# Average pooling on one core: the last two whole-tile stores queued behind the last loads, coarser last parts, and the final wait in a section of its own

## Chip, cores and metric

The kernel runs on one core of a Trainium2 chip. The metric is the device time of one execution in microseconds (us), as a median over several executions. A profile of one execution has a "span", which is 1.7 to 2.4 us shorter than the time. Trace times below are counted from the start of the span. All runs quoted were with a granted clock of 1.0.

## The reference, cut to what matters

```python
# x: 32 x 128 x 256 x 256 float32, kernel_size = 2, stride = 2
for i in range(h_out):
    for j in range(w_out):
        window = x[:, :, 2*i : 2*i + 2, 2*j : 2*j + 2]
        output[:, :, i, j] = np.mean(window, axis=(2, 3))
```

Each output is the mean of four inputs. The kernel reads 1073.74 MB, writes 268.44 MB, and does four operations for each output.

## The kernel before

A "unit" is 128 output rows, one for each partition: 256 KB read and 64 KB written. There are 4096 units. They are handled as 127 whole tiles of 32 units (tiles 0 to 126) and a last tile 127, cut into parts of 16, 8, 4 and 4 units so that the work after the last load is short. SP issues the loads into two input buffers. DVE (VectorE) adds the two rows of each pair, then the two columns. ACT (ScalarE) multiplies by 0.25 and issues the store. There are two result buffers for whole tiles and a third for tile 127.

```python
def take(engine, sem, n=1):            # wait for a semaphore and count it down
    engine.wait_ge(sem, n)
    engine.sem_inc(sem, -n)

def sums(it, dst):                     # DVE: two adds for each tile or part
    dve.tensor_add(out=it[:, :, 0:w], in0=it[:, :, 0:w], in1=it[:, :, w:]).then_inc(halfway)
    take(dve, halfway)
    dve.tensor_add(out=dst, in0=it[:, :, 0:w:2], in1=it[:, :, 1:w:2]).then_inc(summed)

def tile_sums(b):
    take(dve, stored[b], 16)           # the store out of this result buffer has landed
    take(dve, loaded[b], 16)
    sums(ins[b], res[b])
# ... SP: loads of tiles 0 to 126, each when its buffer is free, then:
        for a, b, part in parts:       # tile 127 in parts of 16, 8, 4, 4 units
            sp.dma_start(out=it[:, a:b], in_=...).then_inc(part, 16)
        take(sp, held)                 # tile 126 scaled
        sp.dma_start(out=ot[whole - 1], in_=res[(whole - 1) % 2]).then_inc(tail, 16)
# ... ACT: scale and store of tiles 0 to 125, then:
        take(act, summed)
        scale(res[(whole - 1) % 2], held)
        for a, b, _ in parts:
            take(act, summed)
            scale(dst[:, a:b])
            take(act, scaled)
            act.dma_start(out=..., in_=dst[:, a:b]).then_inc(tail, 16)
        take(sp, tail, 16 * (len(parts) + 2))      # all stores of the end have landed
```

## Time and profile before

| quantity | value | where it is from |
|---|---|---|
| time, median of the first 3 runs | 3103.62 us (3103.59 to 3103.67) | timed runs |
| span of the profiled run | 3101.5 us | page header |
| rate over the span | 433 GB/s | page, DMA part |
| DVE and ACT busy | 54% and 15% | page, part 1 |
| last store issued by ACT | 3095.98 us | timeline |
| last increment of the last store | 3100.42 us | trace's semaphore records |

In the traces a whole-tile load or store is 128 packet records (and 16 of 4 bytes each), and each transfer gives its semaphore 16 increments (those of the last load part of before came from 3089.29 to 3090.51 us). The page counts 16 DMA engines, and I read one increment as the end of one engine's share; "landed" means the sixteenth increment. A "piece" is one packet record of the trace: 64 KB for a whole-tile load and 16 KB for a whole-tile store. The lines are shown in the prediction.

### The profile page before, as it was taken

What the parts mean: (1) busy time and instruction counts of PE and PEld (TensorE: products, weight loads), DVE (VectorE), ACT (ScalarE), POOL (GpSimd) and SP (SyncE); (2) the same over time, 40 slices, a digit from 0 to 9 for tenths busy, and PEclk for the clock granted to TensorE, in tenths of its full rate; (3) what the DMA queues carried; (4) which work ended last, traced back from release to release, by engine and by line L of the source; (5) the groups of instructions that cost most, each with busy time, mean ns of one, the idle gap of its engine ahead of it and who ended that gap; (6) DMA issues with size and microseconds to landing.
All of it is one profiled execution on the core that took longest, in us unless ns stands there. A gap on an engine that the chain in (4) does not pass through costs nothing. (4 is left out here: it accounts for less than half of the span.)

```text
span 3101.5 us, 2614 instructions
## 1 busy us (share of the span) xinstructions
DVE 1679.6 (54%) x262; ACT 464.7 (15%) x132; POOL 0.2 (0%) x4
## 2 busy tenths in 40 slices
DVE  4555555555555555555555555555555555555556
ACT  1111111111111111111111111111111111111111
POOL 0000000000000000000000000000000000000000
DMA  9999999999999999999999999999999999999999
GB/s 416 436 440 426 436 440 426 437 440 424 438 440 423 439 437 425 440 428 434 440 433 430 442 423 436 439 427 440 435 426 437 439 427 436 438 424 439 437 425 416
DMA packets 37728, 1342.19 MB, mean 433 GB/s; under 512 B 4192, under 2 KB 4192, under 8 KB 4576
## 3 DMA queue, kind: packets, MB, share of 16 engines
q1 hardware_dynamic: 19008, 1075.85, 80.1%
q10 hardware_dynamic: 18720, 266.35, 20.1%
HBM read 1073.74 MB, written 268.44 MB: 433 GB/s over the span
## 5 line engine op out<-in xcount | busy, mean ns | idle before, releaser
L87 DVE TENSOR_TENSOR in_tile<-in_tile 128x8192 f32<-128x8192 f32 (+1 forms) x131 | 1113.0, 8496 | 1396.4 <-DVEq L67 1396.4
L97 ACT ACTIVATE res<-res 128x4096 f32<-128x4096 f32 (+1 forms) x131 | 463.5, 3538 | 2594.8 <-ACTq L67 2594.8
L89 DVE TENSOR_TENSOR res<-in_tile 128x4096 f32<-128x4096 f32 (+1 forms) x131 | 566.8, 4327 | 19.2
L97 ACT ACT_TABLE_LOAD x1 | 1.3, 1283 | 36.3 <-ACTq L67 36.3
L234 POOL MEMSET const-bfloat16-1.0<- 128x1 bf16 x1 | 0.1, 101 | 0.0
L234 POOL MEMSET const-uint8-127<- 128x1 uint8 x1 | 0.1, 101 | 0.0
L234 POOL MEMSET const-float32-0.0<- 128x1 f32 x1 | 0.1, 98 | 0.2 <-issue 0.2
L234 POOL MEMSET const-float32-1.0<- 128x1 f32 x1 | 0.1, 98 | 0.0
## 6 DMA issues: line engine op xcount, KB each, us to landing
out_dram<-res ACTq DMA_DIRECT2D x126, 2048.0 KB, 30.8
in_tile<-in_x_dram SPq DMA_DIRECT2D x1, 4096.0 KB, 22.0
in_tile<-in_x_dram SPq DMA_DIRECT2D x1, 2048.0 KB, 27.1
in_tile<-in_x_dram SPq DMA_DIRECT2D x2, 1024.0 KB, 30.0
out_dram<-res SPq DMA_DIRECT2D x1, 2048.0 KB, 11.7
in_tile<-in_x_dram SPq DMA_DIRECT2D x127, 31.5
out_dram<-res ACTq DMA_DIRECT2D x1, 1024.0 KB, 8.1
out_dram<-res ACTq DMA_DIRECT2D x1, 512.0 KB, 6.0
```

The source lines that it names most:

```text
L87: dve.tensor_add(out=it[:, :, 0:w], in0=it[:, :, 0:w], in1=it[:, :, w:]).then_inc(halfway)
L89: dve.tensor_add(out=dst, in0=it[:, :, 0:w:2], in1=it[:, :, 1:w:2]).then_inc(summed)
L97: act.mul(out=dst, in_=dst, mul=0.25).then_inc(done)
L234: nc = _bacc.Bacc("TRN2", target_bir_lowering=False, num_devices=1)
```

## The change

Its intent is to let the last loads through before anything that can wait. The store of tile 125 leaves ACT's queue, and both it and the store of tile 126 stand on SP's queue behind the last loads. Tile 127 comes in parts of 16, 8 and 8. The final wait moves to a second section in which only SP takes part, so the other engines can finish while the stores drain. (A section is a `with tc.tile_critical()` block of the code. SP leaves it only when the other engines have finished in it, as its waits of 9.6 and 1.7 us below show.)

```diff
-    halfway, summed, scaled, held, tail = ...
+    halfway, summed, scaled, tail = ...
+    held = [sem(f"held{k}") for k in range(2)]
...
-        b = rest if rest - a <= 4 else a + (rest - a) // 2
+        b = rest if rest - a <= 8 else a + (rest - a) // 2
...
-        take(sp, held)
-        sp.dma_start(out=ot[whole - 1], in_=res[(whole - 1) % 2]).then_inc(tail, 16)
+        for k, t in enumerate((whole - 2, whole - 1)):
+            take(sp, held[k])
+            sp.dma_start(out=ot[t], in_=res[t % 2]).then_inc(tail, 16)
...
-        for t in range(1 + 2 * pairs, whole - 1):
-            scale_store(t, t % 2, stored[t % 2] if t < whole - 2 else tail)
-        take(act, summed)
-        scale(res[(whole - 1) % 2], held)
+        for t in range(1 + 2 * pairs, whole - 2):
+            scale_store(t, t % 2, stored[t % 2])
+        for k, t in enumerate((whole - 2, whole - 1)):
+            take(act, summed)
+            if k == 0:
+                act.sem_inc(free[t % 2])
+            scale(res[t % 2], held[k])
...
+    with tc.tile_critical():
         take(sp, tail, 16 * (len(parts) + 2))
```

More of the change, by code (lines that the diff above doesn't have):

```diff
@@ L60, in _pool_2x2 @@
     loaded, free, stored = [[sem(f"{n}{b}") for b in range(2)] for n in ("loaded", "free", "stored")]
-    halfway, summed, scaled, held, tail = [sem(n) for n in ("halfway", "summed", "scaled", "held", "tail")]
+    halfway, summed, scaled, tail = [sem(n) for n in ("halfway", "summed", "scaled", "tail")]
+    held = [sem(f"held{k}") for k in range(2)]
     def take(engine, sem, n=1):
```

## The prediction

> **What bounds the kernel now.** I read the page first, its header and the rows of shares.
>
> ```profile
> span 3101.5 us, 2614 instructions
> DVE 1679.6 (54%) x262; ACT 464.7 (15%) x132; POOL 0.2 (0%) x4
> ...
> DMA  9999999999999999999999999999999999999999
> ...
> q1 hardware_dynamic: 19008, 1075.85, 80.1%
> q10 hardware_dynamic: 18720, 266.35, 20.1%
> ```
>
> No compute engine is near full, while the DMA row is full in all 40 slices and the two queues' packet times add up to 100.2% of sixteen DMA engines' span. q1 is the SP queue (loads, and the one store that SP issues), q10 the ACT queue (stores). The kernel must read 1073.74 MB and write 268.44 MB; at the page's 433 GB/s that alone is 3099.7 us. So in the main loop nothing but bytes counts. The change touches only the last 45 us, so the second view is the table by stretches over the end (columns: stretch, its length, busy time of DVE, ACT and POOL, clock, DMA share, GB/s).
>
> ```profile
> 3067.00:3080.00 13.00, 12.29 (x2) 0.00 (x0) 0.00 (x0) 1.00 1.01 435
> 3080.00:3090.00 10.00, 9.71 (x5) 5.53 (x2) 0.00 (x0) 1.00 0.99 423
> 3090.00:3096.00 6.00, 4.84 (x5) 2.32 (x3) 0.00 (x0) 1.00 1.00 427
> 3096.00:3099.00 3.00, 0.00 (x0) 0.00 (x0) 0.00 (x0) 1.00 0.93 371
> 3099.00:3101.50 2.50, 0.00 (x0) 0.00 (x0) 0.00 (x0) 1.00 0.03 11
> ```
>
> The DMA engines stay full to 3099: the end is a drain of queued bytes, too, and not a wait for arithmetic. Third, the timeline of the last instructions, because DVE is busy almost without a gap there and would be the next bound (columns: start, duration, engine, line, operation).
>
> ```profile
> 3067.57 8.69 DVE L87 TENSOR_TENSOR in_tile<-in_tile 128x8192 f32<-128x8192 f32 x1 [9.71 <-DVEq L67]
> ...
> 3084.66 0.35 SPq L126 DMA_DIRECT2D out_dram<-res  x1
> ...
> 3087.53 2.29 DVE L87 TENSOR_TENSOR in_tile<-in_tile 128x2048 f32<-128x2048 f32 x1
> ...
> 3089.96 1.23 DVE L89 TENSOR_TENSOR res<-in_tile 128x1024 f32<-128x1024 f32 x1
> 3091.10 1.22 DVE L87 TENSOR_TENSOR in_tile<-in_tile 128x1024 f32<-128x1024 f32 x1
> 3091.30 1.06 ACT L97 ACTIVATE res<-res 128x1024 f32<-128x1024 f32 x1 [1.67 <-ACTq L67]
> ...
> 3095.25 0.63 ACT L97 ACTIVATE res<-res 128x512 f32<-128x512 f32 x1 [1.34 <-ACTq L67]
> 3095.98 0.34 ACTq L154 DMA_DIRECT2D out_dram<-res  x1
> ```
>
> From the trace's instruction records: DVE's start at 3067.57 waited last for the store of tile 124 out of the same result buffer (its wait passed at 3067.35; the load had landed at 3065.5). From then on it runs through to 3095.13. The parts of the last tile landed at 3080.0, 3085.6, 3088.0 and 3090.5, and DVE took them up at 3080.75, 3087.53, 3091.10 and 3093.08: every part was there 0.7 to 3.1 us early. The last store is issued at 3095.98, its last increment arrives at 3100.42 and the program ends at 3101.48.
>
> [...] in the packet records a 64 KB load piece (2.418 us) and a 16 KB store piece (0.611 us) alternate. Moving a store from ACT's queue to SP's therefore changes its place, not the capacity. [...] Here 15 of the last 16 increments arrive by 3099.8 and the sixteenth at 3100.42: one engine is behind the rest, and that one sets the end. [...]
>
> **The change part by part.**
>
> *Order of the transfers.* Before, the store of tile 125 goes to ACT's queue at 3061.76 and its 16 KB pieces alternate with the last tile's 32 KB and 16 KB load pieces. In the packet records this store runs from 3066.95 to 3080.2. After, it waits on SP's queue behind the loads. It is 8 pieces on each engine, 8 x 0.611 = 4.9 us, so the loads end about 4.9 us sooner (some 3084.6 in place of 3089.5) and the store takes 3084.6 to 3089.5. The store of tile 126, issued at 3084.66 as before, starts at 3089.5 as before. From there on both kernels have the same bytes left. Bytes moved within a full stretch give nothing back: 0 us. The rate doesn't differ either: a 16 KB piece takes 0.611 us as a load and as a store. DVE gains nothing from earlier parts, since it found each one waiting already: 0 us. The start of DVE at 3067.57 hangs on the store of tile 124, which is untouched: 0 us.
>
> *16, 8, 8 for 16, 8, 4, 4.* Pieces get larger. Per engine, sixteen load pieces of 8 KB at 0.309 us (4.95) become eight of 16 KB at 0.611 (4.89), and sixteen store pieces of 2 KB at 0.084 (1.35) become eight of 4 KB at 0.1595 (1.28): together 0.13 us less DMA time by these durations. Successive 2 KB records start 0.08 us apart on the late engine, so the store part may be nearly nothing; I take 0.1 us. On DVE two pairs of adds become one: before 3091.10 to 3095.13; after, 2.43 us to the second add (3089.96 - 3087.53) and 1.225 us of it, so to 3094.76: 0.38 sooner. ACT's last step then takes 1.06 in place of 0.63, and the issue falls at about 3095.98 + 0.43 - 0.38 = 3096.03: 0.05 later. That is beside the drain: the stores ahead of it (the 1 MB and the first 512 KB one) keep the engines busy until about 3097.4, the late engine until 3098.7. An issued transfer needs about 1.0 us to its first packet (the first load: 0.96 to 1.98), with up to 1.8 us on the last of the engines; so its pieces are ready at 3097.05 to 3097.85. On most engines there is no hole, on some one of up to 0.4 us, but the late engine, which sets the end, has none.
>
> *The second section.* Before, after the last increment SP, ACT and DVE go through the exit of the section (3100.50 to 3100.79 in the records), then all engines through the program's end barrier (to 3101.48): 1.06 us. After, ACT and DVE leave the first section while stores are still draining, and after the wait SP has only its own exit. One semaphore step of some 0.07 us and the round trip to DVE go away: 0.1 us by estimate. The entry of the second section costs nothing visible, as SP then waits for the tail anyway.
>
> Sum: 0 - 0.1 - 0.1 = -0.2 us. From the median of 3103.62 us: 3103.4 us.
>
> **The rivals.** (a) *The last store is on the path as a whole.* It is now 512 KB, and the table of transfers gives longer times for that.
>
> ```profile
> out_dram<-res ACTq DMA_DIRECT2D x1, 512.0 KB, 6.0
> out_dram<-res ACTq DMA_DIRECT2D x2, 256.0 KB, 4.7
> ```
>
> If landing follows from size, the end is at 3096.03 + 6.0 = 3102.0 in place of 3100.42: +1.6 us, some 3105.1. Against it: those 6.0 us are mostly waiting behind other stores; the pieces themselves take 8 x 0.16 = 1.3 us. A hole of 0.4 us on the late engine would be the mild form, 3103.8. (b) *Earlier loads pull DVE forward.* If the parts had been what DVE waits for, a gain of 1 to 2 us of the 4.9 us by which the last load comes earlier would be an estimate, so some 3102. Against it: the landings above, all early. And even so the bytes left would still be drained at 433 GB/s to 3099. (c) *Reads alone and then writes alone run at another rate than mixed.* The table by stretches has 435 for mixed and 423 GB/s for mostly reads. If 20 us of it lost 1%, that would be +0.2 us; but that stretch held the 8 KB pieces, and equal pieces cost the same in both directions.
>
> **Range and chances.** The three times of before lie within 0.08 us, so noise of one chip is small; a hole in the drain (+0.4 to +1.6) and a better exit or better rate (-0.5 to -1) set the range: 3102.5 to 3104.4. A 2% change would be 62 us, and only some 45 us of the program are touched at all, with a drain that can't be shortened: within 2% at 0.99, faster 0.005, slower 0.005.
>
> **What would show it right or wrong.** Right: DMA share near 1.0 up to 3099 again; the last load part landed near 3085.6; the store of tile 125 in 3084.6 to 3089.5; DVE still starting its last whole tile at 3067.6 and now ending near 3094.8; the last issue near 3096.0 and the last increment within 0.3 us of 3100.3; fewer steps between it and the end. Wrong: a stretch of low DMA share between 3097 and 3099 with the last landing past 3101 (rival a), a DVE start other than 3067.6, or a span changed before 3060, where the instructions are the same.

The sum: 0 (order) - 0.1 (parts) - 0.1 (section) = -0.2 us. That the store of tile 125 changes its place and not the capacity rests on the two queues' shares of the page (80.1% and 20.1%) and on the packet records, which can be sorted into sixteen chains by their times. In those chains of before's trace a 16 KB store piece follows a 64 KB load piece in 87% of cases between 100 and 3000 us. The 1.0 to 1.8 us to a first packet are those of before's first load alone: issued at 0.96, with first packets on the sixteen engines at 1.98 to 2.76 us. The 0.07 us of a semaphore step are the distance of two of SP's records at the exit (3100.43 and 3100.50).

## The result and the profile after

The changed kernel took 3103.39 us as a median of 6 runs (3103.22 to 3103.51). Before took 3103.61 us in its 6 runs (3102.92 to 3103.67). The ratio is 1.0000 with a 95% interval of 0.9987 to 1.0013. A ratio is the mean time of one kernel's runs over that of the other's of the same rounds, so it is not quite the ratio of the medians. A difference of 0.2 us lies below what these runs resolve, so from here on the trace has to speak.

The table by stretches of the changed kernel, over the same end (stretch, length, busy time of DVE, ACT and POOL, clock, DMA share, GB/s):

```profile
3067.00:3080.00 13.00, 11.88 (x2) 0.00 (x0) 0.00 (x0) 1.00 0.99 425
3080.00:3090.00 10.00, 9.85 (x4) 5.48 (x2) 0.00 (x0) 1.00 1.02 436
3090.00:3096.00 6.00, 4.86 (x4) 1.82 (x3) 0.00 (x0) 1.00 0.98 416
3096.00:3099.00 3.00, 0.00 (x0) 0.34 (x1) 0.00 (x0) 1.00 0.98 404
3099.00:3101.50 2.50, 0.00 (x0) 0.00 (x0) 0.00 (x0) 1.00 0.07 30
```

The DMA engines are full to 3099 again (share 0.98 in the last 3 us before it). Only what they carry is in another order. The table of transfers on the changed kernel's page shows the order (issuing queue, count, size, median us from issue to landing):

```profile
in_tile<-in_x_dram SPq DMA_DIRECT2D x1, 4096.0 KB, 17.8
in_tile<-in_x_dram SPq DMA_DIRECT2D x2, 2048.0 KB, 24.4
out_dram<-res SPq DMA_DIRECT2D x2, 2048.0 KB, 20.2
```

The 4 MB part landed 17.8 us after its issue, in place of 22.0 us before. The gain is 4.2 us there, and the store of tile 125 pays for it. DVE got nothing from it: the three parts now lay ready for 4.9 to 6.8 us before DVE took them up, after 0.7 to 3.1 us in before. The timeline of the last instructions on DVE and ACT (start, duration, engine, line, operation):

```profile
3067.97 8.69 DVE L88 TENSOR_TENSOR in_tile<-in_tile 128x8192 f32<-128x8192 f32 x1 [9.71 <-DVEq L68]
...
3091.50 2.28 DVE L88 TENSOR_TENSOR in_tile<-in_tile 128x2048 f32<-128x2048 f32 x1
3091.71 1.06 ACT L98 ACTIVATE res<-res 128x1024 f32<-128x1024 f32 x1 [1.66 <-ACTq L68]
...
3095.28 1.06 ACT L98 ACTIVATE res<-res 128x1024 f32<-128x1024 f32 x1 [2.52 <-ACTq L68]
3096.44 0.34 ACTq L159 DMA_DIRECT2D out_dram<-res  x1
```

DVE starts its last whole tile 0.40 us later than in the trace of before (3067.97 against 3067.57), although no instruction ahead of it has changed. It waits last for the sixteenth increment of tile 124's store, which came at 3067.72 in this execution and at 3067.32 in the other. The difference is old by then. The first load landed 0.19 us later than in before, the third 0.39 us later (66.61 against 66.22), and all later ones 0.37 to 0.48 us later. So it arises in the first three loads, where both kernels have the same code. Other executions of the changed kernel and its variants begin with a shift of 0.04 to 0.31 us at the third load (all_three, after_late2, after_late4 below), and two runs with one of 1.8 to 2.1 us (parts_16_16, before_late2). It differs between executions; what sets it stays open. For comparisons of traces I therefore count the end from DVE's start (first two columns), which takes this difference out. Each row is one profiled execution, and the times come from the trace's instruction and semaphore records.

| kernel | DVE start to last issue | DVE start to last increment | last increment to end of span |
|---|---|---|---|
| before | 28.42 | 32.85 | 1.06 |
| changed | 28.47 | 32.79 | 0.98 |

By this measure the change saves 0.06 + 0.08 = 0.14 us. The second section is seen in SP's own list of waits in the changed kernel (waiting engine and line, awaited engine, us, times, longest):

```profile
SPq L107 <- DVEq L107: 9.6, 1, 9.6
SPq L107 <- ACTq L107: 1.7, 1, 1.7
```

SP waits 9.6 and 1.7 us for DVE and ACT to leave the first section. That is time in which it would have waited for the stores anyway. These lines are missing from before, where the exit comes after the last increment.

### The profile page after: what moved, and what is told of

The parts are those of the page before. It is cut to its first block, busy times and chain, and to the rows that moved or that the text cites. A ratio compares the mean times of both kernels' runs of the same rounds, so it can differ in the third digit from the quotient of the medians.

```text
span 3101.7 us, 2612 instructions
## 1 busy us (share of the span) xinstructions
DVE 1679.3 (54%) x260; ACT 464.5 (15%) x131; POOL 0.2 (0%) x4
## 6 DMA issues: line engine op xcount, KB each, us to landing
in_tile<-in_x_dram SPq DMA_DIRECT2D x1, 4096.0 KB, 17.8
```

## The experiments

**First group: the three parts of the change alone, and all of it, on one chip.** The theory is that only bytes, pieces and closing steps count. The rivals are that early loads pull DVE forward, that the size of the last store is on the path, and that reads and writes kept apart run slower.

*order_only* is the kernel before with the new order of stores (parts 16, 8, 4, 4, one section):

```diff
-        take(sp, held)
-        sp.dma_start(out=ot[whole - 1], ...)
+        for k, t in enumerate((whole - 2, whole - 1)):
+            take(sp, held[k])
+            sp.dma_start(out=ot[t], ...)        # and ACT's side of it
```

> Only the order of the stores is changed (tiles 125 and 126 behind the last loads; parts stay 16, 8, 4, 4; one section). Theory of bytes: the DMA engines are full to 3099 us either way, so 0.0 us against before (within 0.1 us), with the last load part landing near 3086 in place of 3090.5 us and nothing gained from it. Rival that early loads pull DVE forward: 1 to 2 us faster. Rival that reads and writes kept apart run slower: about 0.2 us slower.

*parts_only* is the kernel before with the new parts:

```diff
-        b = rest if rest - a <= 4 else a + (rest - a) // 2
+        b = rest if rest - a <= 8 else a + (rest - a) // 2
```

> Only the parts are changed to 16, 8, 8. Theory of bytes: fewer and larger pieces save 0.05 to 0.1 us; the last store is issued within 0.1 us of before and its pieces are already covered by the queue ahead of them. Rival that the last store's size is on the path: 0.4 to 1.6 us slower.

*section_only* is the kernel before with the final wait moved:

```diff
+    with tc.tile_critical():
         take(sp, tail, 16 * (len(parts) + 2))
```

> Only the final wait is moved into a second section of SP alone. Theory: the time from the last increment of the last store to the end goes from 1.06 to about 0.96 us and everything before it is unchanged: 0.1 us faster. Rival that entering the second section costs something: 0.1 us or more slower.

*all_three* is the changed kernel again:

> The whole change again, on the chip of its parts. Theory: the sum of the three, 0.15 to 0.25 us faster than before. If the three parts don't add up to it, one of them acts through another.

Measured, with the trace columns as above:

| kernel | median us (5 runs; before 9) | lowest to highest | ratio, 95% interval | DVE start to last increment | last increment to end |
|---|---|---|---|---|---|
| before | 3103.53 | 3102.55 to 3105.19 | | 32.85 (first chip) | 1.06 (first chip) |
| order_only | 3103.98 | 3102.80 to 3105.09 | 1.0001, 0.9988 to 1.0015 | 32.89 | 1.06 |
| parts_only | 3103.44 | 3103.37 to 3103.55 | 1.0000, 0.9986 to 1.0013 | 32.73 | 1.06 |
| section_only | 3103.50 | 3102.48 to 3103.54 | 0.9999, 0.9985 to 1.0013 | 32.88 | 0.98 |
| all_three | 3103.53 | 3103.43 to 3104.78 | 1.0001, 0.9988 to 1.0015 | 32.79 | 0.98 |

The timed runs decide nothing here. Single executions of one kernel scatter over as much as 2.6 us, and even the whole change shows 0.00 us between medians on this chip, after 0.22 us on the first. The traces, one for each kernel, say more. How far they can be trusted is seen on section_only: nothing before its last increment is changed, and yet it stands 0.03 us from before in that column. The closing steps take 1.06 us in all four traces without the second section (before_late2 below is the fourth), and 0.98 us in seven of the eight with it (1.02 us in the last, wide_loads_16k_stores). The new parts take about 0.1 us off the stretch before: 32.73 to 32.79 us in three traces with them, 32.85 to 32.89 in three without. The order alone adds 0.04 us, about as much as that. The sum is consistent with all_three, so no part was seen to need another one to act. The rival of early loads (1 to 2 us faster) falls on order_only. So does that of separated reads and writes (0.2 us slower), on one trace with a scatter of some 0.03 us.

**Second group: how much room DVE's chain has.** If the end is a drain of queued stores, a delay on DVE is swallowed until it exceeds the room. So I put an idle add on DVE ahead of the last part, in a tile of its own, which is set to zero at the start:

```diff
         for a, b, part in parts:
             take(dve, part, 16)
+            if b == rest:
+                dve.tensor_add(out=idle, in0=idle, in1=idle).then_inc(halfway)
+                take(dve, halfway)
             sums(it[:, a:b], dst[:, a:b])
```

The add has 2048 elements in *before_late2* (kernel before) and *after_late2* (changed kernel), and 4096 in *after_late4*. *parts_16_16* is the changed kernel with two parts, `rest - a <= 16` in place of 8.

> The kernel before with one idle add of 2048 elements on DVE (2.29 us in the trace of before) just ahead of the last part, so that the last store is issued about 2.4 us later (3098.4). Theory of bytes: the late DMA engine was still busy with earlier stores until about 3099.2, and an issue needs 1.0 to 1.8 us to its first packet, so of the 2.4 us only 0.1 to 0.9 us reach the end. Rival that DVE's chain ends the kernel: all 2.4 us reach it.

> The changed kernel with the same idle add ahead of its last part (which is twice as large). Theory: here the last store's 4 KB pieces began at 3099.0 on the late engine and its issue was 0.05 us later, so the slack is about 0.3 to 0.7 us less than in the kernel before and 0.6 to 1.6 us of the 2.4 us reach the end. Rival that DVE's chain ends the kernel: all 2.4 us.

> The changed kernel with an idle add of 4096 elements (4.42 us) ahead of its last part: well past any slack. Theory: of the further 2.13 us over the shorter add nearly all reach the end now, 2.7 to 3.8 us above the changed kernel, with a hole of 2 us or more in the DMA share before the last store. Rival that DVE's chain ends the kernel even without the add: 4.5 us.

> The changed kernel with parts of 16 and 16. The last store is 1 MB, 8 pieces of 8 KB on each engine, 2.48 us, issued about 3096.3 + 0.4 us, with 1.0 to 1.8 us to its first packet. Theory: the queue ahead of it runs dry at about 3097.0 on most engines and 3097.8 on the late one, so a hole of 0.3 to 1.0 us opens and the end is 0.3 to 1.0 us later than in the changed kernel. Rival that landing follows the last store's size and issue: 2 us or more. If the end doesn't move, the queue is deeper than I count.

| kernel | median us (4 runs; before 3103.51 in 7) | DVE start to last issue | last issue to last increment | DVE start to last increment |
|---|---|---|---|---|
| before (first chip) | | 28.42 | 4.43 | 32.85 |
| before_late2 | 3104.73 | 30.85 | 2.01 | 32.86 |
| changed (first chip) | | 28.47 | 4.31 | 32.79 |
| after_late2 | 3104.14 | 30.91 | 2.62 | 33.53 |
| after_late4 | 3106.23 | 33.05 | 2.62 | 35.66 |
| parts_16_16 | 3103.87 | 28.95 | 3.86 | 32.81 |

In before_late2 the issue came 2.43 us later and the last increment 0.01 us later: the whole delay was swallowed. My 0.1 to 0.9 us was too much. In after_late2, 0.74 us of 2.44 reached the end, inside the 0.6 to 1.6 expected. In after_late4 all of the further 2.13 us did. The timed medians of these two, 0.63 and 2.72 us above before's with ranges that don't touch it, agree with the traces (0.60 and 2.73 us more than before from DVE's start to the end of the span), though the ratio's intervals include 1. The stretches of after_late4 show the hole that then opens:

```profile
3097.00:3098.00 1.00, 1.00 (x1) 0.00 (x0) 0.00 (x0) 1.00 0.64 262
3098.00:3099.00 1.00, 0.85 (x2) 0.00 (x0) 0.00 (x0) 1.00 0.05 20
3099.00:3100.00 1.00, 0.56 (x1) 0.32 (x1) 0.00 (x0) 1.00 0.00 0
3100.00:3101.00 1.00, 0.00 (x0) 0.74 (x1) 0.00 (x0) 1.00 0.00 0
3101.00:3102.00 1.00, 0.00 (x0) 0.00 (x0) 0.00 (x0) 1.00 0.31 127
```

When the queue ahead of it had run dry, a store of 256 KB took 2.01 us from issue to last increment and one of 512 KB 2.62 us. So the room follows, as an estimate from these: before 4.43 - 2.01 = 2.4 us, changed 4.31 - 2.62 = 1.7 us. (The 2.01 us come from before_late2 alone, whose delay of 2.43 us uses up just this room; the 2.62 us stand in both after_late2 and after_late4.) The change, which wins 0.14 us, spends 0.7 us of the room. The timed median of before_late2 stands 1.22 us above before (single runs from 3103.41 to 3104.95), which the trace's 0.01 us doesn't show. In its profiled run one DMA engine was further behind than usual (tile 124's sixteenth increment 1.83 us after the fifteenth, 0.83 us in before), and DVE's start with it. This was so from the third load on (1.60 us behind the fifteenth, and the landing 2.05 us later than in before), long before the idle add. Whether that explains the other runs, too, is open; that the delay was swallowed whole rests on this one trace. In the changed kernel's trace the sixteenth increment of a load came 0.05 us after the fifteenth for the first tile, 0.62 us after it half way and 0.84 us at the end, so one engine fell behind under the steady load there, too. The traces don't number the DMA engines, so which one it is isn't known.

parts_16_16 was a miss by the trace. I expected the end 0.3 to 1.0 us later; it is 0.02 us later counted from DVE's start. (The timed runs don't decide it: the median is 0.36 us above before's, and the ranges overlap.) The hole itself is there on most engines, as its stretches show:

```profile
3096.00:3097.00 1.00, 0.00 (x0) 1.00 (x1) 0.00 (x0) 1.00 0.20 82
3097.00:3098.00 1.00, 0.00 (x0) 0.41 (x1) 0.00 (x0) 1.00 0.06 25
3098.00:3099.00 1.00, 0.00 (x0) 0.00 (x0) 0.00 (x0) 1.00 0.66 279
```

The first pieces of its last store began 0.86 to 1.00 us after the issue on the sixteen engines, where I had counted 1.0 to 1.8 us. The path by issue, 28.95 + 3.86 = 32.81 us, then falls on the same moment as the changed kernel's drain on its late engine, 32.79 us. The hole on fifteen engines cost 0.02 us here, within the scatter, while the sixteenth was still behind. It stands at the very edge, though: no room is left.

**Third group: an attempt to beat both kernels.** If time is the sum of the pieces' durations, fewer and larger store pieces should win. *wide_stores* takes the first 126 tiles in pairs, so that each partition holds 64 units and one store covers two tiles in 32 KB pieces:

```diff
-    ot = ov[0:whole * TILE * P].rearrange("(t p g) f -> t p g f", p=P, g=TILE)
+    ot = ov[0:end].rearrange("(t p g) f -> t p g f", p=P, g=2 * TILE)      # xt likewise
-        sp.dma_start(out=ins[b], in_=xt[t]).then_inc(loaded[b], 16)
+        sp.dma_start(out=ins[b], in_=xt[t][:, half(b)]).then_inc(loaded[b], 16)
...
+        big_scale(r)                  # both halves
+        take(act, scaled)
+        act.dma_start(out=ot[t], in_=res[r]).then_inc(stored[r], 16)
```

> The changed kernel, but the first 126 tiles are stored in pairs: one store for two tiles, in pieces of 32 KB on each partition in place of 16 KB. Theory of bytes: the time is the sum of the pieces' durations on each DMA engine. A 16 KB piece takes 0.6107 us and a 32 KB piece 1.2132 us as a load in the trace, so each pair saves 0.008 us, 504 pairs per engine save 4.1 us, and 63 fewer increments of 0.009 us save 0.6 us: some 3099 us, 4 to 5 us under the changed kernel, though the tail of the kernel is the same. Rival that the stores' pieces cost the same per byte at any size, or that a longer turn for stores starves the loads: no gain, or slower.

It took 3163.46 us (3155.67 to 3175.20) against 3103.60 of before, a ratio of 1.0183 (1.0169 to 1.0197). That is within the 2% that the verdict rule calls the same, but clear of noise: the expectation of 4 to 5 us less was wrong by the sign. The profiled run's page:

```profile
span 3173.3 us, 2235 instructions
...
DMA  9999999999999999999999999999999999999999
```

The DMA engines are as full as ever, so it is not a wait that costs. The store pieces did what was expected (1.214 us each; 602.0 us in sum for each DMA engine). The 64 KB load pieces did not: their mean went from 2.420 us to 2.488 us, with one in a hundred above 3.6 us. 1016 of them on each engine make 0.068 x 1016 = 69 us. Two things had changed at once, so *wide_loads_16k_stores* keeps the paired layout of the loads and goes back to a 16 KB store for each tile:

```diff
-        big_scale(r)
-        take(act, scaled)
-        act.dma_start(out=ot[t], in_=res[r]).then_inc(stored[r], 16)
+        for b in range(2):
+            # ... wait for the sum, free the input, scale this half
+            act.dma_start(out=ot[t][:, half(b)], in_=res[r][:, half(b)]).then_inc(stored[r], 16)
```

> The paired layout of wide_stores (each load reads 64 KB pieces that lie 128 KB apart in HBM, in place of one unbroken 8 MB stretch), but again one store per tile in pieces of 16 KB (32 KB apart). If it is the layout of the loads that stretched their pieces (mean 2488 against 2420 ns), the time is again some 3150 us or more and the load pieces are again uneven. If it is the 32 KB store pieces that disturb the loads, the load pieces are back at 2420 ns and the time is within 1 us of 3103.5.

It took 3103.21 us (3103.19 to 3103.48) against 3103.59, ratio 0.9999 (0.9982 to 1.0016), with load pieces at a mean of 2.419 us. So the layout of the loads is not the cause; the 4 MB stores in 32 KB pieces are. Whether through the piece's size or through the burst that follows when a store comes only every second tile, these runs don't separate, and it stays open. Its median is the lowest of all, but the interval doesn't resolve it.

This run is also the clearest test of what ends the kernel. Here the last store out of the result buffer that DVE needs had landed at 3044.45, so DVE waits only for the load of its last whole tile (landed at 3061.39) and starts at 3061.53. The last two rows of its timeline are:

```profile
3088.83 1.06 ACT L104 ACTIVATE res<-res 128x1024 f32<-128x1024 f32 x1 [2.52 <-ACTq L68]
3089.99 0.34 ACTq L168 DMA_DIRECT2D out_dram<-res  x1
```

The last store is issued 6 us earlier than in the other two kernels (3095.98 and 3096.44), and its last increment comes at 3100.46, as in theirs (3100.42 and 3100.76). All arithmetic was over at 3089.9, and the queued bytes still drained to 3100.

## Why the prediction was right

- **The bound.** Full DMA engines to 3099 were predicted and found. (The 3099.7 us "at the page's 433 GB/s" prove nothing, as that rate is the bytes over the span itself; the full DMA row and the 100.2% carry the argument.) wide_loads_16k_stores shows it from the other side: arithmetic 6 us earlier, the same end.
- **The order, 0 us.** The last load part was to land near 3085.6 and landed at 3085.99 in an execution that was 0.40 us behind from its first loads on. The store of tile 125 was to run from 3084.6 to 3089.5; its pieces ran from 3084.3 to 3089.6 on fifteen DMA engines and from 3085.5 to 3090.4 on the late one, which the prediction had not told apart. order_only measured +0.04 us in the trace.
- **The parts, -0.1 us.** DVE was to end 27.19 us after its start (3094.76 - 3067.57) and did (3095.16 - 3067.97 = 27.19). The issue was to come 0.05 us later and did (28.42 to 28.47). parts_only measured -0.12 us, and the changed kernel -0.06 us, with a scatter of some 0.03 us between traces.
- **The section, -0.1 us.** It measured -0.08 us in the traces of the changed kernel, section_only and all_three (wide_loads_16k_stores, which has it too, shows 1.02 us, so -0.04).
- **The sum, -0.2 us.** The trace gives -0.14 us. The timed medians gave -0.22 us on one chip and 0.00 us on another, so the 3103.39 us against the predicted 3103.4 is closer than the argument can claim: that it fits to 0.01 us is luck.
- **Misses inside it.** I named a DVE start other than 3067.6 and a difference before 3060 as signs of error, and a last increment within 0.3 us of 3100.3 as a sign of being right. DVE started at 3067.97, the 0.40 us were there long before 3060, and the last increment came at 3100.76, 0.46 us from 3100.3. All three are the offset from the first three loads, where the code is the same; without it the last increment stands at 3100.36. The mistake was to take times of one execution as fixed to 0.1 us in another. The time from an issue to its first piece was over-estimated: with the queue run dry it was 0.84 to 1.00 us on the sixteen engines (after_late2, the pieces sorted into sixteen chains by their times), not 1.0 to 1.8 us. So the last store had more room than I gave it. The range of 1.9 us held the medians, but single executions of before alone went from 3102.55 to 3105.19, which I had not seen in its first three runs.
- **The rivals.** (a) The last store's size on the path: real only once the room of 1.7 us is used up. Then 512 KB took 2.62 us from issue to landing (after_late2, after_late4), not the 6.0 us of the table. (b) Early loads: order_only shows nothing, and the parts lay ready longer than before. (c) Separate reads and writes: a 16 KB piece took 0.611 us either way, and order_only shows nothing.

## What to carry to other kernels

Here the DMA engines were full until the last microseconds (share 0.93 and 0.98 from 3096 to 3099 us, before and after). The last load part of the changed kernel landed 4.5 us earlier (3085.99 in place of 3090.51), and the order alone moved the end by 0.04 us (order_only's trace). Where a page looks like this, ask how many bytes are left, not which come first. Before cutting or merging the last pieces of work, measure the room between the last issue and the moment at which the queue ahead of it runs dry: in these traces a delay of 2.43 us inside it cost 0.01 us (before_late2), and a further 2.13 us beyond it cost 2.13 us (after_late2 to after_late4). When a change is worth less than the scatter of single executions, compare intervals inside the traces that begin after the disturbance, and take the scatter of such an interval from a kernel in which it was not changed.
